# Where the operands of the split matmuls lie in SBUF: a decoder trunk with high parts moved down and low parts moved up

## The chip, the cores and the metric

The kernel runs on one core of one Trainium2 chip. The metric is the device time of one execution in microseconds (us). TensorE (PE) does the matmuls, VectorE (DVE), ScalarE (ACT) and GpSimd (POOL) the elementwise work, and SyncE (SP) issues most DMA transfers. SBUF is the on-chip memory: each of its 128 partitions is addressed in bytes from 0, and this text gives an address inside a partition in KiB.

## The reference

The computation is a two-layer decoder trunk over 512 tokens of width 1024, all in float32. Layer 0 mixes tokens with a 4-head mLSTM (a gated matrix memory), layer 1 with sliding-window grouped-query attention (16 query heads, 4 key/value heads, window 128, one learned sink per head). Both layers go on in the same way:

```python
x = layer_norm(DEEPNORM_ALPHA * x + mix, mix_ln_g[i], mix_ln_b[i])
x = layer_norm(DEEPNORM_ALPHA * x + squared_relu_mlp(x, mlp_w_up[i], mlp_w_down[i]), mlp_ln_g[i], mlp_ln_b[i])
x = x + jax.nn.sigmoid(x @ ple_w_gate[i] + ple_b_gate[i]) * (p[i] @ ple_w_proj[i])
```

The MLP goes from 1024 to 4096 and back, `square(relu(x @ w_up)) @ w_down`. The mLSTM projects x to queries, keys, values, an output gate and two scalar gates, normalises each head's output, scales it with `a_head_norm_g`, multiplies by the sigmoid of the output gate and projects with `w_out`. Attention projects with `w_q`, shares keys and values from `kv_w`, and projects back with `w_o`.

## The kernel before

**Split products.** Every float32 matrix is kept as two parts in a 32-bit format that TensorE reads at full rate: a high part (names ending in H, h or hi: XH, whi, YH, S1h) and a low part, the rest (XL, wlo, YL, S1l). `split` makes the high part with a cast on ACT and the low part with a subtraction on VectorE. `mm3` computes a product as high x high, high x low and low x high, three matmuls into one PSUM bank. A matmul has a stationary operand, 128 columns that are loaded into the array first, and a moving operand, here mostly 512 columns, that streams past. In `mm3(o, lh, ll, rh, rl, ...)` lh and ll are stationary, rh and rl move. In rows of the profile and of the order the moving operand stands first: `mm<-XH,whi` streams XH past the stationary whi.

**Stages in order.** (1) The mLSTM's projections: value and gate weights w_vo in groups of 412 columns, then w_qk; the first group's weights come through `first_w`. (2) Four heads, each with scores, decay, normalisation, and `mlstm_out`, where GpSimd multiplies by hg, the head-norm scale. Head outputs are transposed into YH and YL. (3) w_out (`xstat_mix`): Y stationary, weights moving, two halves of 512 output columns, in each half four token tiles of 128 rows and four weight chunks of 512 KB. Each tile's PSUM bank is added to the residual res0 to res3, and after the second half `ln_finish` normalises a tile (aggregate the statistics, the power -0.5 on GpSimd, two passes over 1024 columns on VectorE), transposes it on TensorE and splits it into XH and XL. (4) The MLP, in four quarters: an up-projection of 1024 hidden columns with the weights stationary (`wstat`; XH and XL move), then the down-projection as seven block products instead of eight matmuls of blocks, with sums of blocks of hidden values (sets A11, A12, S1, S23, S4A) stationary and sums of weight blocks moving. (5) The gate with the per-layer embedding (`ple`), X stationary. (6) In layer 1 keys and values, then the query projection with attention per block, whose output overwrites the queries in QS; w_o with QS stationary in two halves, the second of them with `ln_finish` as in (3); the MLP and the gate again.

**What sets the order.** The program is written stage by stage, but a planner with its own estimates of durations rearranges each engine's instructions before the launch; the resulting list of each engine is fixed, and the engine goes through it strictly in order, waiting at an instruction whose inputs or buffers are not ready. DMA transfers are issued in the same way from lists on SP (weights, residual input, output) and POOL (broadcast vectors).

**Buffers.** Pools are opened and closed on a stack on the left side (growing up from address 0) or on the right side (growing down from 224 KiB). `wpool` on the left holds 3 raw weight chunks (wraw), 6 whi and 6 wlo; every weight except part of w_down passes through it. A pool opened where a closed one was waits for that one's last users.

## Time and profile before

| | before |
|---|---|
| time, median of 3 runs (lowest, highest) | 1205.97 us (1205.9, 1207.38) |
| profiled execution: time | 1205.88 us |
| profiled execution: span of its instructions | 1204.2 us |
| mean granted TensorE clock | 0.995 |
| busy: TensorE, VectorE, ScalarE, GpSimd | 1180.2, 878.7, 584.3, 95.0 us |
| instructions | 15638 |

The span runs from the first to the last instruction of the profiled execution; the time lies 1.7 us above it. Times in views are us from the span's start. A view of groups gives the busy time, the mean duration in ns, and the idle time just before; TensorE overlaps consecutive matmuls, so the distance from one start to the next, not the duration, says what a matmul costs.

### The profile page before, as it was taken

What the parts mean: (1) busy time and instruction counts of PE and PEld (TensorE: products, weight loads), DVE (VectorE), ACT (ScalarE), POOL (GpSimd) and SP (SyncE); (2) the same over time, 40 slices, a digit from 0 to 9 for tenths busy, and PEclk for the clock granted to TensorE, in tenths of its full rate; (3) what the DMA queues carried; (4) which work ended last, traced back from release to release, by engine and by line L of the source; (5) the groups of instructions that cost most, each with busy time, mean ns of one, the idle gap of its engine ahead of it and who ended that gap; (6) DMA issues with size and microseconds to landing.
All of it is one profiled execution on the core that took longest, in us unless ns stands there. A gap on an engine that the chain in (4) does not pass through costs nothing.

```text
span 1204.2 us, 15638 instructions
## 1 busy us (share of the span) xinstructions
PE 1180.2 (98%) x5918; PEld 1003.1 (83%) x5918; DVE 878.7 (73%) x1454; ACT 584.3 (49%) x1015; POOL 95.0 (8%) x189
## 2 busy tenths in 40 slices
PE   8999999999999999999999999989999999999998
PEld 8899998888888888888788998879888888888877
DVE  7555556877488589599785888596847848959974
ACT  4445552565464463564343555346645536346431
POOL 1011020100000000001201332110000000000100
PEclk9999999999999999999999999989999999999999
DMA  7322227214405306115242211161350440621511
GB/s 243 105 85 67 82 88 265 85 36 134 146 1 175 105 23 199 59 53 171 69 135 74 71 37 36 66 214 36 93 170 18 140 140 1 192 88 36 157 54 53
DMA packets 34843, 120.35 MB, mean 100 GB/s; under 512 B 3968, under 2 KB 4752, under 8 KB 34768
## 3 DMA queue, kind: packets, MB, share of 16 engines
q1 hardware_dynamic: 32688, 112.26, 29.3%
q0 software_dynamic: 2080, 7.09, 1.9%
q8 instruction: 46, 0.75, 0.3%
q14 instruction: 29, 0.24, 0.1%
HBM read 117.24 MB, written 2.10 MB: 99 GB/s over the span
## 4 chain that ended last, share of the span: by engine, by line
PE 88%; DVE 7%; ACT 2%; issue 1%; DMA 1%; SPq 0%; ACTq 0%; DVEq 0%
PE mm L90 28%; PE mm L89 28%; PE mm L88 28%; DVE wlo L77 1%; PE tp L128 1%; ACT pr L878 1%; DMA wraw<-in_w_vo_dram 1%; DVE QS L848 1%; DVE smax L865 1%; PE tp L88 1%; DVE sc L864 1%; PE tp L89 1%; PE tp L90 1%; ACT whi L76 1%; DVE pr L882 0%
## 5 line engine op out<-in xcount | busy, mean ns | idle before, releaser
L77 DVE TENSOR_TENSOR wlo<-wraw,whi 128x1024 fp32r<-128x1024 f32 (+1 forms) x168 | 204.0, 1217 | 130.0 <-ACT whi L76 129.1
L76 ACT CAST whi<-wraw 128x1024 fp32r<-128x1024 f32 (+1 forms) x168 | 173.9, 1037 | 251.8 <-PE mm L90 134.0
L89 PE MATMUL mm<-XL,whi 128*128 128x512 f32 (+1 forms) x640 | 237.1, 371 | 2.2 <-DVE XL L133 2.2
L88 PE MATMUL mm<-XH,whi 128*128 128x512 f32 (+1 forms) x640 | 237.2, 372 | 1.2 <-ACT ot L226 0.9
L90 PE MATMUL mm<-XH,wlo 128*128 128x512 f32 (+1 forms) x640 | 236.6, 370 | 0.0
L88 PE MATMUL mm<-whi,XH 128*128 128x512 f32 (+2 forms) x424 | 146.2, 346 | 3.9 <-DVE q L838 2.2
L89 PE MATMUL mm<-wlo,XH 128*128 128x512 f32 (+2 forms) x424 | 145.1, 343 | 0.0
L90 PE MATMUL mm<-whi,XL 128*128 128x512 f32 (+2 forms) x424 | 144.5, 344 | 0.0
L89 PEld LDWEIGHTS mm<-XL,whi 128*128 128x128 f32 x640 | 122.2, 191 | 22.1 <-DVE XL L133 2.5
L88 PEld LDWEIGHTS mm<-XH,whi 128*128 128x128 f32 x640 | 122.0, 192 | 21.8 <-ACT ot L226 1.3
L90 PEld LDWEIGHTS mm<-XH,wlo 128*128 128x128 f32 x640 | 122.0, 191 | 20.1
L76 ACT CAST whi<-rb 128x1024 fp32r<-128x1024 f32 x80 | 84.0, 1050 | 101.2 <-PE mm L89 56.7
L77 DVE TENSOR_TENSOR wlo<-rb,whi 128x1024 fp32r<-128x1024 f32 x80 | 97.4, 1222 | 39.1 <-ACT whi L76 39.1
L88 PEld LDWEIGHTS mm<-whi,XH 128*128 128x128 f32 x424 | 80.0, 189 | 13.0 <-DVE q L838 3.9
L89 PEld LDWEIGHTS mm<-wlo,XH 128*128 128x128 f32 x424 | 80.2, 189 | 7.7 <-issue 1.5
L90 PEld LDWEIGHTS mm<-whi,XL 128*128 128x128 f32 x424 | 80.1, 189 | 6.5 <-issue 0.8
L89 PE MATMUL mm<-wlo,S23h 128*128 128x512 f32 x128 | 50.7, 396 | 0.0
L89 PE MATMUL mm<-wlo,S4Ah 128*128 128x512 f32 x128 | 50.6, 396 | 0.0
L88 PE MATMUL mm<-whi,S23h 128*128 128x512 f32 x128 | 50.6, 396 | 0.0
L88 PE MATMUL mm<-whi,S4Ah 128*128 128x512 f32 x128 | 50.6, 395 | 0.0
L90 PE MATMUL mm<-whi,S4Al 128*128 128x512 f32 x128 | 50.3, 396 | 0.0
L635 DVE TENSOR_TENSOR res<-res,mm 128x512 f32<-128x512 f32 x72 | 48.6, 682 | 1.5 <-PE mm L90 1.0
(354 smaller groups left out, 2228.8 us busy)
## 6 DMA issues: line engine op xcount, KB each, us to landing
wraw<-in_w_up_dram SPq DMA_DIRECT2D x64, 512.0 KB, 3.7
rb<-in_w_down_dram SPq DMA_DIRECT2D x48, 512.0 KB, 4.4
wraw<-in_w_down_dram SPq DMA_DIRECT2D x16, 512.0 KB, 3.6
wraw<-in_w_gate_dram SPq DMA_DIRECT2D x16, 512.0 KB, 3.7
wraw<-in_w_vo_dram SPq DMA_DIRECT2D x18, 412.0 KB, 3.3
wraw<-in_w_qk_dram SPq DMA_DIRECT2D x8, 512.0 KB, 4.3
wraw<-in_w_out_dram SPq DMA_DIRECT2D x8, 512.0 KB, 3.8
wraw<-in_w_q_dram SPq DMA_DIRECT2D x8, 512.0 KB, 4.0
```

The source lines that it names most:

```text
L76: ACT.copy(hi, raw)
L77: eng.tensor_sub(lo, raw, f32(hi))
L88: PE.matmul(o, lh, rh, start=start, stop=False)
L89: PE.matmul(o, lh, rl, start=False, stop=False)
L90: PE.matmul(o, ll, rh, start=False, stop=stop)
L128: PE.transpose(pt[:, tsl(j)], src[:, tsl(b + j)], ident)
L635: V.tensor_add(r[:, h], r[:, h], bank)
L848: V.tensor_sub(QS[other, hs, tsl(t)], pv[own], f32(QS)[own, hs, tsl(t)])
L864: V.copy_predicated(cur, mk, prev)
L865: V.tensor_reduce(smax[:, :, pr], cur, AX.X, ALU.max)
L878: ACT.activation(pt_[:, par, pr, :], scs[pr][:, par, :], AF.Exp, scale=ASCALE, bias=nm[:, par, pr:pr + 1], accum_out=sm[:, par, pr:pr + 1])
```

## The change

The operands change places; the arithmetic stays as it is. A new pool, `upper`, on the right side takes wraw, wlo and XL. XH and whi stay at the left. YH and YL, the sets of the seven products, the queries QS, and keys and values move from the right side to the left; the residual tiles, the broadcast vectors, the ring of raw weights and hidden values, and the temporary T stand on the right. Addresses by the allocation of the two programs, in KiB of a partition:

| operand | before | after |
|---|---|---|
| XH | 4 to 20 | 4 to 20 |
| XL | 20 to 36 | 172 to 188 |
| whi | 50 to 74 | 22 to 46 |
| wlo | 74 to 98 | 200 to 224 |
| YH, YL | 192 to 224 | 46 to 78 |
| sets of the seven products, layer 0 | 180 to 220 | 46 to 102 |
| sets of the seven products, layer 1 | 114 to 154 | 46 to 102 |
| QS | 114 to 146 | from 46 up |
| weights of the second half of w_out and of w_o | as whi, wlo | 116 to 148 |

Sorted by where the two operands lie (high means from 112 KiB up), and by moving columns, the split matmuls number:

| columns | both low | only stationary high | only moving high | both high |
|---|---|---|---|---|
| 512 before | 1992 | 1824 | 0 | 12 |
| 512 after | 1752 | 664 | 1400 | 12 |
| 412 before | 480 | 0 | 0 | 0 |
| 412 after | 160 | 160 | 160 | 0 |
| 256 before | 816 | 0 | 0 | 320 |
| 256 after | 400 | 272 | 363 | 101 |

Beside that, the second half of w_out and of w_o gets a pool of its own for four whi and four wlo (xhi, xlo) instead of sharing the six of wpool; the first w_vo transfer is issued on ACT's queue instead of SP's; and a one-column copy by GpSimd, which reads the gates' first result, holds back the transfer of hg.

```diff
+    upper = pool("upper", side="right")

-    def load_w(src, n, eng=V):
-        raw = wpool.tile([P, 1024], F32, tag="raw", name="wraw", bufs=3)
-        hi = wpool.tile([P, 1024], F32R, tag="whi", name="whi", bufs=6)
-        lo = wpool.tile([P, 1024], F32R, tag="wlo", name="wlo", bufs=6)
+    def load_w(src, n, room=None):
+        raw = upper.tile([P, 1024], F32, tag="raw", name="wraw", bufs=3)
+        hi, lo = (room.tile([P, 1024], F32R, tag=f"x{x}", name=f"x{x}", bufs=4) if room else
+                  (wpool if x == "hi" else upper).tile([P, 1024], F32R, tag=f"w{x}", name=f"w{x}", bufs=6) for x in ("hi", "lo"))

-    XL = base.tile([P, KD, S], F32R, name="XL")
+    XL = upper.tile([P, KD, S], F32R, name="XL")

     def xstat_mix(wname, xh, xl, alpha, g, b):
+        wctx = ExitStack()
+        room = pool("wroom0", stack=wctx, side="right", reuse_waits="tile")
         for half in range(2):
-            w = [load_w(A[wname][half, c], 1024) for c in range(4)]
+            w = [load_w(A[wname][half, c], 1024, room if half else None) for c in range(4)]
...
+        wctx.close()

-    py = pool("py", stack=yctx, side="right", reuse_waits="tile")
+    py = pool("py", stack=yctx, side="left", reuse_waits="tile")

     def first_w(g, k0, n):
-        raw = wpool.tile([P, 1024], F32, tag="raw", name="wraw", bufs=3)
+        raw = upper.tile([P, 1024], F32, tag="raw", name="wraw", bufs=3)
-        lo = wpool.tile([P, 1024], F32R, tag="wlo", name="wlo", bufs=6)
+        lo = upper.tile([P, 1024], F32R, tag="wlo", name="wlo", bufs=6)
-        nc.sync.dma_start(raw[:, :m], A["w_vo"][g, k0 // 2, :, (k0 % 2) * GW:(k0 % 2) * GW + m])
+        (nc.scalar if k0 == 0 else nc.sync).dma_start(raw[:, :m], A["w_vo"][g, k0 // 2, :, (k0 % 2) * GW:(k0 % 2) * GW + m])

     qk_head(1)
+    GP.tensor_copy(hg[:, :1], gsb[:, 0, 0, :1])
     nc.gpsimd.dma_start(hg, A["a_head_norm_g"].partition_broadcast(P))

-    pres = pool("pres", stack=rctx, side="left", reuse_waits="tile")
+    pres = pool("pres", stack=rctx, side="right", reuse_waits="tile")
-    open_mid("left")
+    open_mid("right")

     def seven_pools(i, side):
-        sp["s"] = pool(f"ring{i}", stack=sctx7, side=side, reuse_waits="tile")
+        sp["s"] = pool(f"ring{i}", stack=sctx7, side="right", reuse_waits="tile")
-        sp["T"] = ps.tile([P, 2, 512], F32, name="T")
+        sp["T"] = sp["s"].tile([P, 2, 512], F32, name="T")

-    c7 = seven_pools(0, "right")
-    mlp(0, "right")
+    c7 = seven_pools(0, "left")
+    mlp(0, "left")
     ple(0, False)
     c7.close()
+    qctx = ExitStack()
+    pq = pool("pq", stack=qctx, side="left", reuse_waits="tile")
+    QS = pq.tile([P, QH, S], F32R, name="QS")
-    pk = pool("pk", stack=kctx, side="right", reuse_waits="tile")
+    pk = pool("pk", stack=kctx, side="left", reuse_waits="tile")
...
-    w = [load_w(A["w_o"][1, c], 1024) for c in range(4)]
+    wctx = ExitStack()
+    room = pool("wroom1", stack=wctx, side="right", reuse_waits="tile")
+    w = [load_w(A["w_o"][1, c], 1024, room) for c in range(4)]
     for t in range(NT):
         w_o(t, 1)
         ln_finish(t, sts[t], g, b)
+    wctx.close()
     qctx.close()
```

Not shown: the same move of wraw and wlo in `two`, `ops` and `embed`, and T1's users, which stay.

The planner's lists change with it. On SP's queue, at the end of w_out's weight loads (wraw are raw weight chunks, res0 to res3 the residual tiles), before:

```order
L83 DMA wraw_1918<-in_w_out_dram 128x1024
L83 DMA wraw_1924<-in_w_out_dram 128x1024
L83 DMA wraw_2153<-in_w_up_dram 128x1024
L83 DMA wraw_2159<-in_w_up_dram 128x1024
L83 DMA wraw_2165<-in_w_up_dram 128x1024
L83 DMA wraw_2171<-in_w_up_dram 128x1024
L471 DMA res0_1755<-in_x_dram 128x1024
```

and after:

```order
L84 DMA wraw_1919<-in_w_out_dram 128x1024
L84 DMA wraw_1925<-in_w_out_dram 128x1024
L476 DMA res0_1759<-in_x_dram 128x1024
L476 DMA res1_1760<-in_x_dram 128x1024
L476 DMA res2_1761<-in_x_dram 128x1024
L476 DMA res3_1762<-in_x_dram 128x1024
L84 DMA wraw_1931<-in_w_out_dram 128x1024
```

The residual's four transfers now stand ahead of the last chunk of w_out's second half (wraw_1931) and of the first chunks of w_up.

On TensorE near the end of w_out, second half (mm_1937, mm_1986, mm_2035 and mm_2084 are the banks of tiles 0 to 3, xhi_1932 and xlo_1933 the last chunk), after:

```order
L89 MATMUL mm_1937<-xhi_1932,YH_98 128x512
L90 MATMUL mm_1937<-xlo_1933,YH_98 128x512
L91 MATMUL mm_1937<-xhi_1932,YL_99 128x512
L90 MATMUL mm_1986<-xlo_1933,YH_98 128x512
L91 MATMUL mm_1986<-xhi_1932,YL_99 128x512
L89 MATMUL mm_1986<-xhi_1932,YH_98 128x512
L90 MATMUL mm_1986<-xlo_1933,YH_98 128x512
L91 MATMUL mm_1986<-xhi_1932,YL_99 128x512
L90 MATMUL mm_2035<-xlo_1933,YH_98 128x512
L91 MATMUL mm_2035<-xhi_1932,YL_99 128x512
L89 MATMUL mm_2035<-xhi_1932,YH_98 128x512
L90 MATMUL mm_2035<-xlo_1933,YH_98 128x512
```

where before tile 0 (mm_1930) and tile 1 (mm_1979) were finished one after the other:

```order
L88 MATMUL mm_1930<-whi_1925,YH_95 128x512
L89 MATMUL mm_1930<-wlo_1926,YH_95 128x512
L90 MATMUL mm_1930<-whi_1925,YL_96 128x512
L88 MATMUL mm_1979<-whi_1907,YH_95 128x512
L89 MATMUL mm_1979<-wlo_1908,YH_95 128x512
L90 MATMUL mm_1979<-whi_1907,YL_96 128x512
L88 MATMUL mm_1979<-whi_1907,YH_95 128x512
```

Before, tile 0's last matmul is followed by 72 more of w_out; now the first three tiles end five or six rows apart, and 34 matmuls of w_out follow tile 0's last one.

On VectorE in the normalisation that follows (L155 and L156 add a tile's bank to the residual, L144/L145 and L145/L146 are the two normalising passes), before:

```order
L169 BN_STATS lst_1770<-res0_1755 128x6
L169 BN_STATS lst_1773<-res3_1758 128x6
L155 SCALAR_TENSOR_TENSOR res1_1756<-res1_1756,mm_1979 128x512
L141 BN_AGGR mv_1957<-lst_1770 128x2
L169 BN_STATS lst_1771<-res1_1756 128x6
L136 TENSOR_SCALAR rs_1959<-mv_1957 128x1
L144 SCALAR_TENSOR_TENSOR res0_1755<-res0_1755,mv_1957,bc_1766 128x1024
L141 BN_AGGR mv_2006<-lst_1771 128x2
L145 SCALAR_TENSOR_TENSOR res0_1755<-res0_1755,rs_1959,bc_1768 128x1024
L136 TENSOR_SCALAR rs_2008<-mv_2006 128x1
L144 SCALAR_TENSOR_TENSOR res1_1756<-res1_1756,mv_2006,bc_1766 128x1024
```

and after:

```order
L156 SCALAR_TENSOR_TENSOR res0_1759<-res0_1759,mm_1937 128x512
L156 SCALAR_TENSOR_TENSOR res1_1760<-res1_1760,mm_1986 128x512
L78 TENSOR_TENSOR wlo_2411<-wraw_2409,whi_2410 128x1024
L172 BN_STATS lst_1774<-res0_1759 128x6
L156 SCALAR_TENSOR_TENSOR res2_1761<-res2_1761,mm_2035 128x512
L172 BN_STATS lst_1775<-res1_1760 128x6
L78 TENSOR_TENSOR wlo_2458<-wraw_2456,whi_2457 128x1024
L142 BN_AGGR mv_1964<-lst_1774 128x2
L172 BN_STATS lst_1776<-res2_1761 128x6
L142 BN_AGGR mv_2013<-lst_1775 128x2
L137 TENSOR_SCALAR rs_1966<-mv_1964 128x1
```

The adds of tiles 0 to 2, with two weight splits between them, now come ahead of the first normalising pass, where before tile 0's and tile 1's passes ran ahead of tile 2's add.

On VectorE between attention and the second half of w_o (mm_7284 and mm_7333 are the banks of tiles 0 and 1, L78 is a split's subtraction), after:

```order
L943 BN_STATS lst_6888<-res3_1762 128x6
L78 TENSOR_TENSOR xlo_7280<-wraw_7278,xhi_7279 128x1024
L78 TENSOR_TENSOR wlo_7519<-wraw_7517,whi_7518 128x1024
L78 TENSOR_TENSOR wlo_7525<-wraw_7523,whi_7524 128x1024
L78 TENSOR_TENSOR wlo_7531<-wraw_7529,whi_7530 128x1024
L78 TENSOR_TENSOR wlo_7537<-wraw_7535,whi_7536 128x1024
L154 TENSOR_TENSOR res0_1759<-res0_1759,mm_7284 128x512
L154 TENSOR_TENSOR res1_1760<-res1_1760,mm_7333 128x512
L78 TENSOR_TENSOR wlo_7767<-wraw_7765,whi_7766 128x1024
L943 BN_STATS lst_6885<-res0_1759 128x6
```

and before:

```order
L77 TENSOR_TENSOR wlo_7269<-wraw_7267,whi_7268 128x1024
L77 TENSOR_TENSOR wlo_7507<-wraw_7505,whi_7506 128x1024
L153 TENSOR_TENSOR res3_1758<-res3_1758,mm_7204 128x512
L937 BN_STATS lst_6880<-res3_1758 128x6
L77 TENSOR_TENSOR wlo_7513<-wraw_7511,whi_7512 128x1024
L153 TENSOR_TENSOR res0_1755<-res0_1755,mm_7273 128x512
L153 TENSOR_TENSOR res1_1756<-res1_1756,mm_7322 128x512
L937 BN_STATS lst_6877<-res0_1755 128x6
L937 BN_STATS lst_6878<-res1_1756 128x6
L141 BN_AGGR mv_7300<-lst_6877 128x2
```

The half's last split and four of w_up now stand in one run ahead of tile 0's add.

More of the change, by code (lines that the diff above doesn't have):

```diff
@@ L480, in two @@
         for c in range(2):
-            r = sp["s"].tile([P, 1024], F32, tag="rb", name="rb", bufs=6) if src[2] else wpool.tile([P, 1024], F32, tag="raw", name="wraw", bufs=3)
+            r = sp["s"].tile([P, 1024], F32, tag="rb", name="rb", bufs=6) if src[2] else upper.tile([P, 1024], F32, tag="raw", name="wraw", bufs=3)
             nc.sync.dma_start(r, src[0][src[1] + c])
@@ L497, in ops @@
                 hi = wpool.tile([P, 1024], F32R, tag="whi", name="whi", bufs=6)
-                lo = wpool.tile([P, 1024], F32R, tag="wlo", name="wlo", bufs=6)
+                lo = upper.tile([P, 1024], F32R, tag="wlo", name="wlo", bufs=6)
                 split(raw[c], 1024, hi, lo)
@@ L695, in embed @@
     def embed(i, ph, pl):
-        raw = wpool.tile([P, 1024], F32, tag="raw", name="wraw", bufs=3)
+        raw = upper.tile([P, 1024], F32, tag="raw", name="wraw", bufs=3)
         nc.sync.dma_start(raw, A["pT"][i])
@@ L772, in yoco_kernel @@
     psum_pools(sctx, tp=1, sc=3, pt=2)
-    qctx, bctx = ExitStack(), ExitStack()
-    pq = pool("pq", stack=qctx, side="left", reuse_waits="tile")
-    QS = pq.tile([P, QH, S], F32R, name="QS")
+    bctx = ExitStack()
     pb = pool("pb", stack=bctx, side="right", reuse_waits="tile")
```

2 lines of the change are left out of this document (1 added, 1 removed).

## The prediction

> **What bounds the kernel now.** I read the page's busy times and the shares of the chain first, then the table by stage, then single matmul starts, and last the waits at the places where TensorE stands still.
>
> ```profile
> PE 1180.2 (98%) x5918; PEld 1003.1 (83%) x5918; DVE 878.7 (73%) x1454; ACT 584.3 (49%) x1015; POOL 95.0 (8%) x189
> PE 88%; DVE 7%; ACT 2%; issue 1%; DMA 1%; SPq 0%; ACTq 0%; DVEq 0%
> ```
>
> TensorE is busy for 1180 of 1204.2 us, so only two things can move the time much: the length of a matmul, or one of the few places where TensorE stands. For the length, seven clean stretches of the table by stage (their idle time is zero; a few counts include a neighbour that reaches in):
>
> ```profile
> core 0: us, PE busy (x) PEld busy (x) DVE busy (x) ACT busy (x) POOL busy (x), PEclk, DMA share, GB/s
> 312.15:355.71 43.56, 43.56 (x194) 36.05 (x193) 27.84 (x40) 22.72 (x37) 0.00 (x0) 1.00 0.17 54
> 355.71:395.06 39.35, 39.35 (x170) 31.67 (x169) 31.26 (x42) 18.59 (x22) 0.00 (x0) 1.00 0.50 153
> 933.54:972.58 39.04, 39.04 (x170) 31.67 (x169) 31.13 (x42) 18.57 (x22) 0.00 (x0) 1.00 0.49 156
> 972.58:1016.10 43.52, 43.52 (x194) 36.04 (x193) 27.87 (x40) 22.70 (x37) 0.00 (x0) 1.00 0.18 54
> 1165.88:1192.75 26.87, 26.87 (x122) 22.25 (x120) 13.00 (x19) 5.38 (x8) 0.00 (x0) 1.00 0.13 50
> ```
>
> In a name like mm<-XH,whi the moving operand stands first and the stationary one second. Rows one and four are up-projections, 192 matmuls of 512 columns each with the weights stationary: 43.56 / 192 = 226.9 ns and 226.7 ns. Rows two and three are seven-product stages, 168 matmuls of the same shape with the activation sets S and A stationary: 39.35 / 168 = 234.2 ns in layer 0 and 232.4 ns in layer 1. By the kernel's allocation all operands of the up-projections lie at or below 98 KiB of a partition, and the sets lie at 180 to 220 KiB (layer 0) and 114 to 154 KiB (layer 1). That it is the place and not the role of the activations shows the last row, the layer-1 gate: XH is stationary there too, but at 4 KiB, and 118 matmuls take 227.7 ns. DMA share does not order the five rows (0.50 and 0.49 give 234.2 and 232.4). So a stationary operand in the upper part costs 7.3 or 5.6 ns a matmul, mean 6.4, at full clock.
>
> **The addresses.** Before, 1824 matmuls of 512 columns read a high stationary (sets, YH and YL, QS) and none has a high moving operand beside a low stationary. The allocation after gives 664 of 512 columns and 160 of 412 with a high stationary (wlo in the up-projections and others, XL in the first products), so 1000 fewer: 1000 x 6.4 ns = **-6.4 us**. A further 272 of 256 columns get one. Newly, 1400 of 512, 160 of 412 and 363 of 256 columns have a high moving operand (XL, or wlo, beside a low stationary), which the trace never shows. The nearest rows have both operands high:
>
> ```profile
> 132.06 0.39 PE L88 MATMUL tp<-qkh,qkh 128*128 128x512 f32 x1
> 132.29 0.40 PE L89 MATMUL tp<-qkl,qkh 128*128 128x512 f32 x1
> 132.53 0.39 PE L90 MATMUL tp<-qkh,qkl 128*128 128x512 f32 x1
> 132.76 0.35 PE L88 MATMUL mm<-whi,XH 128*128 128x412 f32 x1
> ...
> 672.76 0.28 PE L860 MATMUL sc<-KL,QS 128*128 128x256 f32 x1
> 672.88 0.28 PE L859 MATMUL sc<-KH,QS 128*128 128x256 f32 x1
> 673.00 0.28 PE L860 MATMUL sc<-KL,QS 128*128 128x256 f32 x1
> ...
> 675.60 0.28 PE L89 MATMUL mm<-wlo,XH 128*128 128x256 f32 x1
> 675.72 0.28 PE L90 MATMUL mm<-whi,XL 128*128 128x256 f32 x1
> 675.84 0.28 PE L88 MATMUL mm<-whi,XH 128*128 128x256 f32 x1
> ```
>
> Three high-high matmuls take 0.70 us, 233 ns each: no more than a high stationary alone. At 256 columns high-high is 120 ns and low-low 120 ns. I therefore take zero for a high moving operand and for the 272 short ones. Bounds: a lone high stationary between two low ones may cost anything from 0 to 6.4 ns (gain 11.7 to 6.4 us on 824 and 1824), and a high moving operand 0 to 6.4 ns (1560 x 6.4 = 10.0 us against).
>
> **The start.** The first products wait for weights while the 512 KB of the head-norm scale share the DMA engines; the change sends that transfer after the first gates (it is first used by the head outputs, some 40 us later) and puts the first weight load on ACT's queue, ahead of nothing but its table load.
>
> ```profile
> 4.90 0.98 PE L256 MATMUL mm<-whi,XH 128*128 128x412 f32 x4 [0.39 <-DVE whi L242]
> 9.23 0.98 PE L256 MATMUL mm<-whi,XH 128*128 128x412 f32 x4 [1.59 <-DVE whi L242]
> ...
> 14.17 0.99 PE L256 MATMUL mm<-whi,XH 128*128 128x412 f32 x4 [0.22 <-ACT XH L233]
> ```
>
> ```profile
> wraw<-in_w_up_dram SPq DMA_DIRECT2D x64, 512.0 KB, 3.7
> ...
> wraw<-in_w_vo_dram SPq DMA_DIRECT2D x18, 412.0 KB, 3.3
> ```
>
> 2.2 us of idle are at stake. By the two DMA rows 100 KB more take 0.4 us longer to land, so the scale's 512 KB are worth 2.0 us of transfer, of which the part before the second stall's load lands at 8.7 us can count: I take **-0.8 us**, bounds -2.0 and 0.
>
> **The w_out tail.** After the last w_out matmul the first up-projection needs tiles 0 and 1 normalised, transposed and split.
>
> ```profile
> 220.79 0.47 PE L90 MATMUL mm<-whi,YL 128*128 128x512 f32 x1
> ...
> 223.89 0.63 PE L128 MATMUL tp<-ident,res 128*128 128x128 f32 x4 [0.85 <-DVE res L145]
> 225.63 0.63 PE L128 MATMUL tp<-ident,res 128*128 128x128 f32 x4 [1.11 <-DVE XL L133]
> 226.01 0.36 PE L89 MATMUL mm<-XL,whi 128*128 128x256 f32 x1
> ```
>
> ```profile
> 206.21 0.69 DVE L155 SCALAR_TENSOR_TENSOR res<-res,mm 128x512 f32<-128x512 f32 x1
> 206.81 1.88 DVE L169 BATCH_NORM_STATS2 lst<-res 128x6 f32<-128x512 f32 x3
> 208.76 0.69 DVE L155 SCALAR_TENSOR_TENSOR res<-res,mm 128x512 f32<-128x512 f32 x1
> ...
> 213.15 1.28 DVE L144 SCALAR_TENSOR_TENSOR res<-res,mv,bc 128x1024 f32<-128x1024 f32 x1
> ...
> 216.87 1.23 DVE L77 TENSOR_TENSOR wlo<-wraw,whi 128x1024 fp32r<-128x1024 f32 x1
> ...
> 224.79 0.69 DVE L133 TENSOR_TENSOR XL<-tp,XH 128x512 fp32r<-128x512 f32 x1
> ```
>
> Today tile 0 is finished at 206.2, TensorE ends w_out at about 221.3, and the XL matmul starts at 226.0, 4.7 later. In the changed order the last weight chunk of the half is used last for tiles 0 to 2, so tile 0 ends only 34 matmuls (7.7 us) before the end of w_out. From there VectorE's rows run to the split of tile 1's second half: 4 adds and 4 statistics at 0.60, 2 weight splits at 1.13, 7 normalising passes at 1.20, 4 XL splits at 0.60 and 0.7 for the small ones (starts from one row to the next, as above): 2.4 + 2.4 + 2.3 + 8.4 + 2.4 + 0.7 = 18.6 us, ending 10.9 after w_out and the matmul at about 11.0. That is **+6.3 us**; bounds +2 (if a gap in TensorE's own work makes tile 0 early) and +8.
>
> **The w_o tail.** Same shape, in layer 1:
>
> ```profile
> 799.19 0.66 PE L128 MATMUL tp<-ident,res 128*128 128x128 f32 x4 [1.94 <-DVE XL L133]
> 799.91 1.23 PE L88 MATMUL mm<-XH,whi 128*128 128x256 f32 x4
> 803.37 0.58 PE L89 MATMUL mm<-XL,whi 128*128 128x256 f32 x1 [2.23 <-DVE XL L133]
> ```
>
> ```profile
> 795.52 1.21 DVE L77 TENSOR_TENSOR wlo<-wraw,whi 128x1024 fp32r<-128x1024 f32 x1
> 797.24 1.22 DVE L77 TENSOR_TENSOR wlo<-wraw,whi 128x1024 fp32r<-128x1024 f32 x1
> 799.05 1.22 DVE L77 TENSOR_TENSOR wlo<-wraw,whi 128x1024 fp32r<-128x1024 f32 x1
> ```
>
> The half-1 weights' own pool lies where attention's buffers were, so their four splits follow the last attention rows on VectorE, with four w_up splits behind them and ahead of tile 0's add: 8 x 1.13 = 9.0 us in one run, where before the half's splits were spread among attention's. But three w_up splits leave the tail (the rows above). I count one split's length of stall before tile 0 and one more in the chain: **+2.2 us**, bounds 0 and +5.
>
> **Elsewhere.** The half-1 w_o matmuls of tiles 0 to 2 can no longer run between attention's, where TensorE has gaps:
>
> ```profile
> 655.00:755.00 100.00, 94.47 (x717) 88.00 (x716) 81.17 (x215) 54.34 (x199) 31.67 (x78) 1.00 0.15 44
> ```
>
> 5.5 us are idle there, but VectorE, busy for 81 us, sets attention's pace, and the moved matmuls fill the wait for the splits behind it instead; nothing, bounds -1.5 and +1.5. The seven-product ring on the other side and the queries' pool opened earlier add waits on closed pools whose last readers are a stage earlier, and TensorE, busy in 1180 of 1204 us, has that stage's matmuls in front of it while they end; nothing, and up to 1 us if that cover is gone.
>
> Sum: -6.4 - 0.8 + 6.3 + 2.2 = +1.3 us. On the profiled execution's own 1205.9 us (span 1204.2), which is the median of the runs (1205.97), that is **1207.2 us**. What this measurement can tell from no change is about 0.2%, 2.4 us, so this is no change.
>
> **The rivals.** *Any operand counts (slower).* A high moving operand pays as a high stationary does. For: nothing in the trace has one alone. Against: high-high pays once, and not at 256 columns. Price: between half of and the whole 10.0 us; at 0.6 of it +6.0 gives 1213. It decides from 1.1 us above my sum, that is 0.7 ns a moving operand, since 1560 of them are added.
>
> *The tails keep their length (faster).* VectorE is 73% busy and TensorE's order leaves it free before tile 0's end; if w_out's end comes later relative to tile 0 (TensorE waiting for a chunk) or the weights split early free the tail, both tails cost 1 us in all, and lone high stationaries cost half, 3.2 ns: -1000 x 6.4 - 824 x 3.2 - 0.8 + 1.0 = -8.8, giving 1197. For: seven of the ten splits now precede tile 0's add. Against: the row count above.
>
> *Place is not the cause.* The seven products stay at 232 to 234 ns after moving down, for a reason that came with their stage. Then only +7.7 of tails and start are left, 1213.6. Against: the gate row, with XH stationary at 227.7. The Trainium skill, "TensorE: Matmul & The Clock Gate", section "Step-by-step: what each phase is for", says that TensorE has two independent read ports on the SBUF, one for the streaming operand and one for the weight load, so that loading the next weights takes nothing from the running matmul; by that rule no address would show and this rival holds. The trace agrees that loads overlap (1003 us of loads beside 1180 us of matmuls) and disagrees that they are free of place.
>
> **How the numbers follow.** Forecast 0.42; any operand counts 0.19; tails keep their length 0.28; place is not the cause 0.11. The forecast's own range, from its bounds, is 1202 to 1211. The range of all, leaving about 2 in 10 out, is 1197 to 1214. Faster by over 0.2% (under 1203.5): 0.10 of the forecast's chance and nearly all of the third, 0.37. Slower (over 1208.4): 0.13 of the forecast's, the second and the last, 0.41. Same: 0.22.
>
> **What would show it.** Address: the seven-product stretches fall from 39.35 to about 38.1 us (168 x 227), and the up-projections, 192 matmuls of which 64 have a high wlo and 64 a high XL, rise from 43.56 to 44.0; over 44.3 means that XL counts too. Start: the second stall, 1.59, falls below 1. Tails: TensorE's idle time between the end of w_out and the first XL matmul grows from 2.2 to about 8 us, named after VectorE's XL; and from 4.2 to about 6 after w_o. I am wrong if a stage between, above all attention, loses or gains more than 2 us, or if the up-projections stay at 43.5.

## The result: slower by 0.9%, and low places bought nothing

The changed kernel takes 1216.8 us (median of 4 runs, 1214.59 to 1219.53); the kernel before took 1205.93 us (1205.51 to 1207.38). The ratio is 1.0089, 95% interval 1.0065 to 1.0113. The prediction said 1207.2 us, no change, in a range of 1197 to 1214; the result lies above that range, on the side to which it gave a chance of 0.41. The profiled execution of the change is the longest of its four, 1219.53 us with a span of 1217.8 us, so the table below, which cuts the two profiled executions at the same matmuls, sums to 13.6 us, as the spans differ, where the medians differ by 10.9.

| stretch, by starts of matmuls | before | after | difference | predicted |
|---|---|---|---|---|
| start to the last w_out matmul | 220.8 | 223.9 | +3.1 | -0.8, and a share of the -6.4 |
| from there to the first up-projection that reads XL | 5.2 | 10.8 | +5.5 | +6.3 |
| MLP of layer 0, to its last product | 345.9 | 343.5 | -2.4 | a share of the -6.4 |
| gate, keys and values, attention, to the last w_o matmul | 223.7 | 228.5 | +4.8 | 0 |
| from there to the first up-projection that reads XL | 7.8 | 11.5 | +3.7 | +2.2 |
| MLP of layer 1 | 345.2 | 343.6 | -1.7 | a share of the -6.4 |
| layer-1 gate, to the last matmul | 50.5 | 51.0 | +0.5 | 0 |

The table by stage of the change shows what became of the matmuls. The first two and the next two rows are an up-projection and a seven-product stage of layer 0 and of layer 1. An up-projection's row goes from the last matmul of the stage ahead to the first of the stage behind, 193 distances, a seven-product row from its own first to its last, 167 distances. The last two rows are the two tails. All are cut 0.1 us early at both ends:

```profile
core 0: us, PE busy (x) PEld busy (x) DVE busy (x) ACT busy (x) POOL busy (x), PEclk, DMA share, GB/s
318.52:362.69 44.17, 44.17 (x195) 36.19 (x194) 27.89 (x40) 22.85 (x37) 0.00 (x0) 1.00 0.18 57
362.69:401.31 38.62, 38.62 (x169) 31.34 (x168) 31.08 (x41) 18.40 (x22) 0.00 (x0) 1.00 0.50 153
902.09:946.26 44.17, 44.17 (x195) 36.19 (x194) 27.89 (x40) 22.86 (x37) 0.00 (x0) 1.00 0.18 58
946.26:984.88 38.62, 38.62 (x169) 31.35 (x168) 31.07 (x41) 18.42 (x22) 0.00 (x0) 1.00 0.52 154
223.74:234.50 10.76, 6.21 (x30) 4.82 (x29) 10.76 (x17) 4.22 (x7) 4.45 (x4) 0.73 0.87 337
806.49:817.99 11.50, 7.05 (x30) 5.54 (x29) 11.46 (x20) 4.08 (x7) 4.24 (x3) 0.61 0.85 317
```

A seven-product stage now takes 38.62 / 167 = 231.3 ns a matmul: down from 234.3 and 232.4, though every set lies below 102 KiB. An up-projection takes 44.17 / 193 = 228.9 ns: up from 226.8. Two thirds of a seven-product stage's matmuls have both operands in the lower part and should have cost 227. So the place was not what the 6 ns were paid for. The same view of the kernel before, at its two tails:

```profile
220.80:226.03 5.23, 2.89 (x21) 1.95 (x18) 5.23 (x8) 4.34 (x7) 0.35 (x1) 1.00 0.47 122
795.56:803.39 7.83, 3.59 (x23) 2.72 (x21) 7.83 (x13) 5.93 (x8) 1.45 (x1) 0.77 0.61 178
```

VectorE is busy through both tails, before and after; they are longer because it has more to do in them. TensorE does not stand idle for all of that time: its idle time grows from 2.3 to 4.6 us in the first tail and from 4.2 to 4.5 us in the second, and the rest is work, 30 instructions begun instead of 21 and 23, a part of them at half clock (PEclk).

The 4.1 us that the two MLP stretches of the table lose seem for the most part not to be a gain of the addresses: with the own room alone on the kernel before (below) they take 344.4 and 343.3 us, 3.4 us less than before, and with the placement alone 1.0 us less.

### The profile page after: what moved, and what is told of

Its sections match the earlier page's. It is cut to its first block, busy times and chain, and to the rows that moved or that the text cites. A ratio compares the mean times of both kernels' runs of the same rounds, so it can differ in the third digit from the quotient of the medians.

```text
span 1217.8 us, 15638 instructions
## 1 busy us (share of the span) xinstructions
PE 1187.6 (98%) x5918; PEld 1006.1 (83%) x5918; DVE 875.5 (72%) x1454; ACT 589.8 (48%) x1019; POOL 93.1 (8%) x190
## 5 line engine op out<-in xcount | busy, mean ns | idle before, releaser
L78 DVE TENSOR_TENSOR wlo<-wraw,whi 128x1024 fp32r<-128x1024 f32 (+1 forms) x160 | 193.9, 1215 | 130.4 <-ACT whi L77 129.1
L77 ACT CAST whi<-wraw 128x1024 fp32r<-128x1024 f32 (+1 forms) x160 | 165.0, 1033 | 226.1 <-PE mm L91 97.5
L78 DVE TENSOR_TENSOR wlo<-rb,whi 128x1024 fp32r<-128x1024 f32 x80 | 97.2, 1219 | 40.4 <-ACT whi L77 40.4
L91 PE MATMUL mm<-whi,S23l 128*128 128x512 f32 x128 | 49.3, 393 | 0.0
```

Of the source, the lines that this page charges most:

```text
L77: ACT.copy(hi, raw)
L78: eng.tensor_sub(lo, raw, f32(hi))
L91: PE.matmul(o, ll, rh, start=False, stop=stop)
```

## The experiments

### What a place costs: the address map

A kernel of matmuls alone, without the model: one tile of SBUF, chains of 512-column matmuls, nothing else running.

```python
for i in range(n):
    m, s = pat[i % len(pat)]              # KiB of moving and stationary operand
    mo = m * 256 + (i // len(pat) % 2) * 512
    so = s * 256 + (i // len(pat) % 4) * 128
    PE.matmul(ps, big[:, so:so + 128], big[:, mo:mo + 512], start=i == 0, stop=i == n - 1)
```

> This kernel leaves the model out and only times matmuls: one SBUF tile filled with cast input, then chains of 512-column split-format matmuls whose moving and stationary operands lie at chosen addresses (13 x 13 pairs at 4, 20, ... 196 KiB, and the triples high x high, high x low, low x high of the up-projection and of the seven products with the addresses before and after). Distance from start to start at full clock. Theory 1 (a high stationary alone pays): 227 ns wherever the stationary is below 112 KiB, 233 above, whatever the moving operand. Theory 2 (any operand in the upper half pays): 227 only where both are low, 233 elsewhere; the triple of the up-projection after the change then has a mean of 231. Theory 3 (the place is not the cause, the neighbouring work of VectorE, ScalarE or DMA in the seven-product stages is): every cell within 1 ns of 227, and the triples of before and after alike. Theory 4 (how the places of successive operands stand to each other counts, not each place alone): the triples give what the traces show, 226.9 and 229.1 for the up-projection before and after, 233.3 and 231.3 for the seven products, while the grid is not a sum of a row and a column effect.

The table by stage of this kernel: first most of the grid, then the triples of the up-projection before, of the layer-0 products before, and of the products after, 48 matmuls each, all with operands within 5 KiB of where the two programs have them:

```profile
50.00:466.77 416.77, 416.77 (x1840) 345.09 (x1839) 0.00 (x0) 0.00 (x0) 0.00 (x0) 1.00 0.00 1
466.77:477.65 10.88, 10.88 (x49) 9.01 (x48) 0.00 (x0) 0.00 (x0) 0.00 (x0) 1.00 0.00 0
553.81:564.69 10.88, 10.88 (x49) 9.01 (x48) 0.00 (x0) 0.00 (x0) 0.00 (x0) 1.00 0.00 0
575.57:586.45 10.88, 10.88 (x49) 9.01 (x48) 0.00 (x0) 0.00 (x0) 0.00 (x0) 1.00 0.00 0
```

10.88 / 48 = 226.7 ns in each triple, and each full-clock cell of the grid, from 8 to 200 KiB on either side, lies between 226.6 and 226.7 but for one that came right after the first (228.9). Theories 1 and 2 are out: no part of SBUF between 8 and 200 KiB is slow. So is theory 4 in its form of KiB places, since the triples are alike. That left the neighbours' work (theory 3) or something that this kernel had made equal for all operands. It had: all its addresses leave 128 when divided by 256.

### What an offset costs: the offset map

The same loop with byte addresses: 13 x 13 fine offsets, and triples at the byte addresses of the two programs (but wlo after stands 8 KiB below its place and the low part of the layer-0 set 4 KiB above; the remainders are the programs' own).

```diff
-    m, s = pat[i % len(pat)]
+    m, s, dm, ds = pat[i % len(pat)]      # byte addresses and steps
+    mo = (m - BASE + (j % 2) * dm) // 4
+    so = (s - BASE + (j % 4) * ds) // 4
```

> As the address map, but with the fine offset of the operands varied: 13 x 13 offsets from 0 to 480 bytes for the moving and the stationary operand at 8 and 64 KiB, a few pairs with one operand at 192 KiB, and triples at exactly the byte addresses that the two programs give to their operands (before, XH, XL, whi and wlo all leave 128 when divided by 512, the layer-1 sets 0, the layer-0 sets and Y 480; after, whi and XH leave 128, the sets 0, XL and wlo 480). In the address map all offsets left 128 and every cell took 226.7 ns. Theory 5 (the operands' offsets to each other count, not the part of SBUF): cells with unlike offsets take 230 to 235 ns and equal ones 226 to 227; the triples give the traces' values within 1 ns: up-projection 226.9 before and 229.1 after, seven products 234.3 and 232.4 before and 231.2 after, second half of w_out in its own room 233.3. Theory 3 (the neighbouring engines' work): all cells and triples stay at 226.7.

The table by stage; the rows are, in order, the triples of the up-projection before, the up-projection after, the products before in layer 0 and in layer 1, the products after, and w_out after with its weights in their own room:

```profile
533.27:544.15 10.88, 10.88 (x49) 9.01 (x48) 0.00 (x0) 0.00 (x0) 0.00 (x0) 1.00 0.01 2
544.15:555.15 11.00, 11.00 (x49) 9.00 (x48) 0.00 (x0) 0.00 (x0) 0.00 (x0) 1.00 0.00 0
555.15:566.39 11.24, 11.24 (x49) 9.04 (x48) 0.00 (x0) 0.00 (x0) 0.00 (x0) 1.00 0.01 1
566.39:577.54 11.15, 11.15 (x49) 9.04 (x48) 0.00 (x0) 0.00 (x0) 0.00 (x0) 1.00 0.00 0
577.54:588.65 11.11, 11.11 (x49) 9.00 (x48) 0.00 (x0) 0.00 (x0) 0.00 (x0) 1.00 0.00 0
610.99:622.19 11.20, 11.20 (x49) 9.01 (x48) 0.00 (x0) 0.00 (x0) 0.00 (x0) 1.00 0.00 0
```

Divided by 48: 226.7, 229.2, 234.2, 232.3, 231.5 and 233.3 ns, where the model's traces have 226.9, 228.9, 234.3, 232.4, 231.2 and 233.3. VectorE and ScalarE stand still here and the DMA engines all but still (a share of 0.01 at most), so theory 3 is out too: the operands' offsets to each other give all of it. The grid, sorted by the difference of the two addresses (moving less stationary) modulo 256 bytes, for the differences that are multiples of 32, from the starts in the trace, without the first cell (half clock) and without the first distance of each cell:

```
difference   cells   mean ns (least to most)
   0          20     227.6   (226.6 to 231.2)
  32          16     233.2   (233.1 to 233.4)
  64          20     229.0   (228.5 to 229.8)
  96          16     233.3   (232.5 to 233.8)
 128          20     232.8   (231.6 to 233.4)
 160          16     234.2   (234.0 to 234.7)
 192          20     233.3   (232.8 to 233.4)
 224          16     233.1   (232.2 to 233.4)
```

The cells of difference 0 that lie above 227 are, all but one, chains that had not settled: each cell has only 12 matmuls and follows one of another difference. The distances in ns of three of them, moving and stationary remainder ahead:

```
128, 128   227 226 227 227 226 227 227 226 227 227 226
 64,  64   236 224 231 236 228 233 231 226 227 227 226
 16,  16   230 232 231 231 231 231 231 232 231 230 232
```

The second starts irregularly and falls into the pattern of the first at its eighth distance; the third, the one exception, does not. The same with the operands far apart (moving at 8 KiB, stationary at 192 KiB, both leaving 128): 233 236 224 231 236 228 232 231 and then 227 227 226.

Before, 2004 of 3828 matmuls of 512 columns had difference 0, 912 had 128 (layer-1 sets and QS) and 912 had 160 (layer-0 sets and Y), because these happened to lie in pools that start at other remainders. After, 676 have 0, and the rest 96, 128, 160 and 224: XL, wlo and the own room leave 224, the sets, YH and QS leave 0, XH and whi leave 128. In a chain that changes its difference from one matmul to the next the price is not the mean of the cells (the up-projection after mixes 0, 96 and 160 and takes 229.2, their cells' mean would be 231.7), which is why mixing hid half of it.

### The kernel before with equal offsets

```diff
     YL = py.tile([P, KD, S], F32R, name="YL")
+    V.memset(py.tile([P, 24], F32, name="ypad"), 0.0)
...
     res[:] = [pres.tile([P, D], F32, name=f"res{t}") for t in range(NT)]
+    V.memset(pres.tile([P, 32], F32, name="rpad"), 0.0)
...
         sp["T"] = ps.tile([P, 2, 512], F32, name="T")
+        if side == "right":
+            V.memset(ps.tile([P, 24], F32, name="spad"), 0.0)
```

> The kernel before with three pads of 96, 128 and 96 bytes, so that sets, YH, YL and QS leave 128 when divided by 256, as XH, XL, whi and wlo do already; the sets and Y stay above 112 KiB. Theory 5 (equal offsets): all 3828 matmuls of 512 columns take 226.7 ns, the seven-product stages fall from 39.35 and 39.04 to 38.1 us, and 1824 x 6.5 ns = 11.9 us come off: 1193.7 us. Theories 1 and 2 (the upper part pays): nothing changes, 1205.5 within 1 us.

1196.47 us (5 runs, 1194.55 to 1196.83), ratio to the kernel before 0.9921 (0.9908 to 0.9935). The table by stage, an up-projection and a seven-product stage of each layer, cut as above:

```profile
308.39:352.13 43.74, 43.74 (x195) 36.22 (x194) 27.87 (x40) 22.86 (x37) 0.00 (x0) 1.00 0.18 57
352.13:389.99 37.86, 37.86 (x169) 31.35 (x168) 30.98 (x41) 18.48 (x22) 0.00 (x0) 1.00 0.50 157
881.47:925.21 43.74, 43.74 (x195) 36.22 (x194) 27.87 (x40) 22.86 (x37) 0.00 (x0) 1.00 0.18 57
925.21:963.07 37.86, 37.86 (x169) 31.35 (x168) 30.98 (x41) 18.48 (x22) 0.00 (x0) 1.00 0.50 157
```

37.86 / 167 = 226.7 ns, the same as the up-projections, with the sets still at 114 KiB and above. Three pads of 96, 128 and 96 bytes give what the placement was to give. The span fell by 11.4 us (1204.2 to 1192.8) against 11.9 expected, but this profiled execution is the shortest of its five; the medians fell by 9.4, and where the other 2.5 went stays open.

### The placement alone

The changed kernel with neither own room nor start edits: those two parts of the diff are taken back.

> The placement alone: neither own room nor start edits. If the placement gains nothing on TensorE (seven products 233 to 231 ns, up-projections and gates 227 to 229) and the other two parts cost what is named for them, the time is that of before within 3 us, 1203 to 1209. If the placement itself brings the delays (waits of pools, order of ScalarE and VectorE), it is 1212 or more.

1207.41 us, ratio 1.0014 (1.0005 to 1.0024): slower by 1.8 us, less than the 0.2% that the prediction took for no change. TensorE's MLP stretches are 344.6 and 345.5 us against 345.9 and 345.2, so what the products gain the up-projections and gates pay. The w_o tail is 5.8 instead of 7.8 us, and from the MLP's end to the last w_o matmul TensorE takes 226.8 us instead of 223.7. The view of TensorE's waits from the end of the layer-0 MLP to the end of w_o, placement alone:

```profile
PE mm L89 <- DVE q L840: 3.0, 7, 0.6
PE sc L861 <- ACT pr L880: 1.6, 1, 1.6
...
PE mm L89 <- DVE kv L809: 0.8, 1, 0.8
```

and before:

```profile
PE mm L88 <- DVE q L838: 2.2, 4, 0.7
...
PE sc L859 <- ACT pr L878: 0.2, 1, 0.2
```

Three waits of attention grew by 0.8, 1.4 and 0.8 us (the third is not listed before): 3.0 of the 3.1. Whether it is the pools' waits or the planner's other order that makes each of them late was not told apart.

### The placement with equal offsets

The same, with two pads, of 96 bytes above everything on the right side and of 128 bytes in a pool on the left:

```diff
+    toppad = pool("toppad", side="right")
     upper = pool("upper", side="right")
...
+    upad = toppad.tile([P, 24], F32, name="upad")
+    V.memset(upad, 0.0)
+    lpad = small.tile([P, 32], F32, tag="lpad", name="lpad", bufs=1)
+    V.memset(lpad, 0.0)
```

> The placement alone (no own room, no start edits) with the same two pads. Theory 5: 13.8 us off the 1207.4 of the placement alone: 1193.6, the same as the aligned kernel before within 2 us, since the place itself is worth nothing. If low places for high parts have a worth of their own, it is below the aligned kernel before by more than 2 us.

1195.86 us, ratio 0.9919 (0.9905 to 0.9933). 11.5 us came off the placement alone, where 13.8 had been expected. Its stages take what those of the aligned kernel before take:

```profile
309.08:352.83 43.75, 43.75 (x195) 36.23 (x194) 28.07 (x40) 22.82 (x38) 0.00 (x0) 1.00 0.18 57
352.83:390.68 37.85, 37.85 (x169) 31.34 (x168) 30.78 (x41) 18.51 (x22) 0.00 (x0) 1.00 0.50 158
```

Once the offsets are equal, no difference is seen by which operands lie low: 1195.9 and 1196.5 us, and the intervals overlap.

### The whole change with equal offsets

The same two pads on the whole change.

> The change with two pads of 96 and 128 bytes, so that all operands of its 512-column matmuls leave 128 when divided by 256; placement, own room and start edits stay. Theory 5: mean distance 230.3 to 226.7 ns on 3828 matmuls, 13.8 us off 1216.8: 1203. If a high place costs anything by itself, the stretches stay above 228 ns and the time above 1208.

1208.46 us, ratio 1.0023 (1.0014 to 1.0033). 8.3 us came off of the 13.8 expected. By the number alone this is the sign named for a place that costs something (above 1208), but the stages say otherwise: every up-projection and every seven-product stage of its trace takes 226.7 ns from start to start, as in the other two aligned kernels. (The spans of the two profiled executions differ by 12.6 us, 1217.8 to 1205.2, but they are the longest of four and the shortest of nine.) The granted clock is 0.988 to 0.991 in its nine executions and 0.989 to 0.994 in the four of the change; how much of the missing 5.5 us that makes was not told apart. What is left above the aligned placement alone, 12.6 us, is own room and start edits, since nothing else differs between the two.

### Without the own room

> The change without the own room of the second-half weights of w_out and w_o (they share wpool's buffers again); placement and start edits stay. If the own room is what makes the two tails long (from the last w_out matmul to the first up-projection that reads XL 10.8 us after the change against 5.2 before, and 11.5 against 7.8 after w_o), both tails return to about 5 and 8 us and the time falls by about 9 us, to 1208. If the order of the tails comes from the residual's pool and the rest of the new placement, they stay near 11 us and the time within 2 us of 1217.

The edit takes the two `wroom` pools out and hands `load_w` no room. 1211.29 us, ratio 1.0043 (1.0028 to 1.0058): 5.5 us less than the change, where 9 had been expected. The tails are 5.2 us after w_out and 5.8 after w_o, 5.5 and 5.7 shorter than with the room. This profiled execution is 1.8 us behind at w_out's last matmul: TensorE's half-clock window after the start lasts 6.8 us in it and 3.4 in the change.

Attention is 1.6 us shorter as well (226.9 against 228.5), but that is not the room's own. In the trace of the change a half-clock window of 3.4 us lies in attention, behind a wait for ScalarE:

```profile
679.27 0.58 PE L865 MATMUL sc<-KH,QS 128*128 128x256 f32 x1 [1.64 <-ACT pr L884]
```

```profile
674.00:686.00 12.00, 9.98 (x71) 9.61 (x70) 8.04 (x24) 5.84 (x23) 3.10 (x8) 0.86 0.26 86
```

At half clock 3.4 us lose up to 1.7 (0.86 over the 12 us of the second row), about the difference. The same window stands in the kernel without start edits (228.4 us); there is none in attention without the room, in the placement alone, or in the aligned whole change, which has the room and takes 226.3 us (equal offsets take 0.6 off this stretch in the other two pairs). The wait itself is 1.6 us in the placement alone too. What decides whether the clock drops behind it these runs do not show.

### The own room alone

The same edit on the kernel before: `load_w` with a room, the two pools, nothing else.

> The kernel before with the own room of the second-half weights alone, no operand moved but these. If the own room by itself lengthens the tails (5.2 to 10.8 us after w_out, 5.8 to 11.4 after w_o, 1.5 us in attention, as removing it from the change showed), the time is 1213 to 1217. If it needs the new placement too, 1204 to 1208.

1211.14 us, ratio 1.0041 (1.0025 to 1.0058), between the two times that had been expected. The tails are 10.3 and 11.4 us, as in the change, but attention is 224.0 as before, and w_out itself ends 1.7 us earlier than before. So the room makes the tails long by itself (5.1 and 3.6 us more), and the 1.5 us in attention that I had expected of it were not its own. TensorE's waits there, by the view of waits over the whole span:

```profile
PE tp L128 <- DVE res L145: 4.0, 3, 3.2
PE tp L128 <- DVE mv L141: 3.4, 1, 3.4
PE mm L88 <- ACT XH L132: 3.0, 6, 1.3
```

The transposes of the normalised tiles wait for VectorE, which goes through the adds, statistics and normalising passes of the four tiles. In the change the w_out tail reads like this on TensorE (L129 transposes a tile):

```profile
223.85 0.40 PE L91 MATMUL mm<-xhi,YL 128*128 128x512 f32 x1
227.45 1.06 PE L129 MATMUL tp<-ident,res 128*128 128x128 f32 x8 [3.20 <-DVE mv L142]
...
230.67 1.22 PE L89 MATMUL mm<-XH,whi 128*128 128x256 f32 x4 [0.87 <-ACT XH L133]
...
233.03 1.94 PE L129 MATMUL tp<-ident,res 128*128 128x128 f32 x8 [0.28 <-DVE res L146]
234.62 0.56 PE L90 MATMUL mm<-XL,whi 128*128 128x256 f32 x1
```

and on VectorE from tile 0's add on (L146 is a second normalising pass, L134 an XL split):

```profile
216.35 0.69 DVE L156 SCALAR_TENSOR_TENSOR res<-res,mm 128x512 f32<-128x512 f32 x1 [0.82 <-PE mm L91]
...
231.65 1.23 DVE L146 SCALAR_TENSOR_TENSOR res<-res,rs,bc 128x1024 f32<-128x1024 f32 x1
232.80 0.68 DVE L134 TENSOR_TENSOR XL<-tp,XH 128x512 fp32r<-128x512 f32 x1
...
234.66 0.68 DVE L134 TENSOR_TENSOR XL<-tp,XH 128x512 fp32r<-128x512 f32 x1
```

Tile 0's add starts 7.5 us before w_out's last matmul starts, and VectorE runs from there with 0.5 us of idle time. The XL split of 232.80 is done at 233.5, but the XL matmul stands in TensorE's list behind the eight transposes of the next tile, which wait for the pass of 231.65. Half-clock windows add to it: PEclk is 0.73 in this tail and 0.61 in the one after w_o (table by stage, first section), against 1.00 and 0.77 before.

### The start edits: without them, and alone

> The change without the two start edits (the head-norm scale is loaded early again, the first weight chunk is issued on SP's queue); placement and own room stay. If these edits cause the late first matmul (5.65 us against 4.90) and the 2.9 us stall at 31 us behind ScalarE's extra table loads, the time falls by 4 to 5 us, to about 1212. If the planner orders ScalarE so because of the new pools, the stall stays and the time is within 2 us of 1217.

1214.4 us, ratio 1.0067 (1.0046 to 1.0088): 2.4 us less than the change, where 4 to 5 had been expected, and the two intervals overlap. In the profiled executions w_out ends 3.4 us earlier.

> The kernel before with the two start edits alone (late head-norm scale, first weight chunk on ACT's queue). If the edits by themselves lead to the late first matmul and the stall behind ScalarE's table loads, the time is 1207.5 to 1210. If they save what the prediction gave them, 1204.7. If the stall after the change needs the new placement too, within 1 us of 1205.5.

Both start edits alone on the kernel before: 1210.73 us, ratio 1.0039 (1.0023 to 1.0054), so they need nothing of the placement to be a loss. Which of the two it is:

```diff
+    GP.tensor_copy(hg[:, :1], gsb[:, 0, 0, :1])
     nc.gpsimd.dma_start(hg, A["a_head_norm_g"].partition_broadcast(P))
```

> The kernel before with the late head-norm scale alone. If the late transfer leads the planner to put ScalarE's cosine behind the gates' tanh, with two more table loads ahead of the copies that free TensorE's banks, the stall at 31 us grows from 0.9 to about 2.9 us, a half-clock window follows it, and the time is 1208 to 1210, nearly all of what both start edits cost (1210.7). If the stall needs the other edit, within 1 us of 1205.5.

The late scale alone: 1210.88 us, ratio 1.0033 (1.0021 to 1.0045). And the other:

```diff
-        nc.sync.dma_start(raw[:, :m], A["w_vo"][g, k0 // 2, :, (k0 % 2) * GW:(k0 % 2) * GW + m])
+        (nc.scalar if k0 == 0 else nc.sync).dma_start(raw[:, :m], A["w_vo"][g, k0 // 2, :, (k0 % 2) * GW:(k0 % 2) * GW + m])
```

> The kernel before with the first weight chunk on ACT's queue alone. The first matmul starts at 5.65 instead of 4.90 us, at half clock, but the 1.6 us stall at 9.2 goes: the time stays within 1 us of 1205.5. If this edit is the costly one, 1208 or more.

1206.57 us, ratio 1.0002 (0.9992 to 1.0011): nothing. The loss is the late scale's. TensorE's longest wait in the kernel with the late scale alone, by the view of waits, and ScalarE's timeline around it:

```profile
PE mm L88 <- ACT ot L226: 2.9, 1, 2.9
```

```profile
30.45 1.28 ACT L303 ACT_TABLE_LOAD   x1
...
32.77 1.28 ACT L445 ACT_TABLE_LOAD   x1
34.06 0.23 ACT L445 ACTIVATE cos<-ang 128x32 f32<-128x32 f32 x1
34.20 0.82 ACT L226 COPY ot<-mm 128x148 f32<-128x148 f32 x4
35.03 1.28 ACT L309 ACT_TABLE_LOAD   x1
```

In the kernel before the cosine came behind the sine without a table load of its own, ahead of the gates' tanh, and the copies that free the banks started at 31.85:

```profile
27.55 0.22 ACT L445 ACTIVATE cos<-ang 128x32 f32<-128x32 f32 x1
...
28.87 1.28 ACT L303 ACT_TABLE_LOAD   x1
...
31.85 0.82 ACT L226 COPY ot<-mm 128x148 f32<-128x148 f32 x4
```

Now the planner puts it behind the tanh: two more table loads, one of them ahead of the copies, which start at 34.20. In the change itself the wait is as long, and a half-clock window follows the idle time:

```profile
34.40 0.79 PE L89 MATMUL mm<-XH,whi 128*128 128x512 f32 x1 [2.88 <-ACT ot L230]
34.99 0.63 PE L90 MATMUL mm<-XL,whi 128*128 128x512 f32 x1
35.42 0.63 PE L91 MATMUL mm<-XH,wlo 128*128 128x512 f32 x1
```

The last two start 0.43 us apart where 0.23 is usual. The transfer itself did little harm and no good. The second stall of the first products, 1.59 us before, is gone in the change, but the first matmul starts later and four take 1.71 us instead of 0.98:

```profile
5.65 1.71 PE L260 MATMUL mm<-whi,XH 128*128 128x412 f32 x4 [1.14 <-DVE whi L246]
...
14.58 0.91 PE L260 MATMUL mm<-whi,XH 128*128 128x412 f32 x4
```

The row of 14.58 stood at 14.17 before. So most of the loss comes behind it, with the copy that holds the transfer back: with it in the program the planner gave ScalarE another order. Why it did stays open.

## Why the prediction was wrong, step by step

**The address term, -6.4 us: wrong in its cause.** The failing step is the sentence that it is "the place and not the role of the activations", drawn from the gate's row. The row was right and the conclusion was not: XH lies low, but it also leaves the same remainder as whi, 128. All five stretches that I compared had place and offset changing together: everything low left 128, everything high left 0 or 224. The layer-0 and layer-1 products, 234.2 and 232.4 ns at different remainders, were in the same table and said that something finer than high and low was at work; I took their mean.

The sentence that DMA share does not order the five rows is wrong as well: 0.13 to 0.18 stand beside 226.7 to 227.7 ns, 0.49 and 0.50 beside 232.4 and 234.2. Only the offset map, with the DMA engines all but still, put that rival out. Of the rows with both operands high, the scores' had unequal offsets; the triples of qkh and qkl have equal ones, but three matmuls between other shapes are too few to settle: one such triple takes 237, 235 and 232 ns in the aligned kernel before too.

In place of -6.4 the placement gave nothing (1207.4 against 1205.6), and equal offsets give -9.4 on the kernel before (1205.9 to 1196.5) and -11.5 on the placement (1207.4 to 1195.9). Against a forecast of -6.4 the placement as a whole is +1.8 us, attention's waits included; that is the largest part of the 9.6 us by which the sum was off. The up-projections rose to 43.95 us (192 x 228.9 ns), where the prediction had said 44.0, but by luck: that figure was counted for high operands, and what was paid there were offsets of 96 and 160. The seven products fell to 38.85 us (168 x 231.2) and not to 38.1.

**The rivals.** "Place is not the cause" was nearest, with 1213.6 and a chance of 0.11. Its condition nearly held, since the seven products fell only to 231.2 ns, but for another reason than the one named, and it lacked the start and attention. "Any operand counts" came near the size of the address term for the wrong cause. The rule of the Trainium skill that stands there ("TensorE: Matmul & The Clock Gate", "Step-by-step: what each phase is for"), two independent read ports, fits the flat address map; the offset map shows that the distance between matmuls still rises by up to 8 ns with the offset between the loaded and the moving operand. Whether the load or the stream pays, and what conflicts there, no run here shows.

**The w_out tail, +6.3: right in its mechanism, 0.8 too long.** +5.5 us, and VectorE has the rows that were counted: four adds, four statistics, two weight splits, seven passes. The XL matmul starts before the fourth XL split is done, which the sum had ahead of it. The sign named for the tails failed: TensorE's idle time was to grow to 8 and 6 us and is 4.6 and 4.5, because TensorE works through a part of the wait. **The w_o tail, +2.2: mis-sized,** though inside its bounds. It is +3.7 in the change; the own room is worth 3.6 by itself and 5.7 beside the placement, because the placement alone shortens this tail by 2.1.

**The start, -0.8: wrong in sign.** I priced the transfer, which is what the edit moves, and not what its holding copy does to ScalarE's list, which the order of the changed program showed: two more table loads of 1.28 us, one of them ahead of the copies that free TensorE's banks. I had read that list for queues, not for table loads. Measured: +3.4 to w_out's end in the change, +4.8 us alone. The stall is 2.9 us instead of 0.9, and a half-clock window of 3.4 us follows it.

**Attention, 0: missed.** +4.8 us in the change, more than the 2 us that the prediction named as its sign of being wrong. 3.1 of it are the placement's, in three waits. The prediction had put the pools' waits at nothing because TensorE would have other matmuls in front of it; whether these three are the pools' or come of the planner's other order stays open. The rest is the half-clock window behind one of them.

## What to carry to other kernels

When a matmul is a few nanoseconds longer in one stage than in another of the same shape, compare the operands' addresses modulo 256 bytes before anything else; padding the pools so that stationary and moving operands leave the same remainder took 0.8% off a kernel at 98% TensorE busy, and no move between parts of the memory did. A correlation between two stages of one kernel confounds whatever the allocator changed with them: a kernel of bare matmuls that varies one address at a time settles in one run what no view of the trace can. And where a planner orders the engines, price an edit by every list that it reorders, table loads on ScalarE included, not by the transfer that it was written for.

## What the runs showed of the hardware that was not expected

At full clock, chains of 512-column matmuls whose stationary and moving operands have equal addresses modulo 256 bytes settle at 226.7 ns from start to start wherever the operands lie, after up to ten irregular distances where the chain ahead had another difference; at remainder 16 they stayed at 231 for the twelve matmuls of the cell. A difference of 64 bytes costs 2 ns, the other multiples of 32 cost 6 to 8 ns. Mixed chains are not additive: single distances of 224 ns occur in the up-projection triple of the change, beside 231 and 232. At 256 columns the trace before shows no such price: 119.6 ns at equal remainders, 118.5 and 116.9 at differences of 160 and 192, by the allocation and the starts at full clock. What in the chip does this no run here shows.
